# Delta stage of a two-layer bidirectional encoder: the four small-tile phases of the inverse merge grouped into two places of a step

## The chip, the cores and the metric

The kernel runs on one core of a Trainium2 chip. The metric is the device time of one execution in microseconds (us), lower is better; the time given is the median of several executions. Engines are written as in the profile: PE (matrix products), ACT (scalar engine), DVE (vector engine), POOL (GpSimd), SP (the queue that issues most transfers).

## What is computed

Two layers over 2048 tokens of width 1024. Each layer makes one wide input projection, a gated DeltaNet branch that is scanned forward and backward in chunks of 64 tokens, a convolution branch, and a gated merge. The part that the change touches is the chunked delta rule, cut here to what matters:

```python
def gated_delta_chunked(q, k, v, g, beta):
    ...
    lmat = jnp.where(strict, jnp.einsum('bhncd,bhnsd->bhncs', k_beta, k) * decay, 0.0)
    ...
    sol = lax.linalg.triangular_solve(eye + lmat, rhs, left_side=True, lower=True,
                                      unit_diagonal=True)
    ...
    def step(state, inp):
        val_n, kc_n, a_n, qd_n, kd_n, dl_n = inp
        v_new = val_n - jnp.einsum('bhcd,bhde->bhce', kc_n, state)
        o_n = jnp.einsum('bhcd,bhde->bhce', qd_n, state) + jnp.einsum('bhcs,bhse->bhce', a_n, v_new)
        state = state * dl_n[..., None, None] + jnp.einsum('bhcd,bhce->bhde', kd_n, v_new)
        return state, o_n
    ...
o = o_fwd + o_bwd
```

The kernel works on chunks of 128 tokens and needs, for each chunk, head and direction, the inverse of a unit triangular 128x128 matrix. Its 32x32 diagonal blocks have been inverted earlier; the delta stage merges them, first to 64x64 and then to 128x128 blocks.

## The kernel before, in words

**The stage.** `delta` runs 16 steps per layer. Step s treats chunk s forward (direction 0) and chunk 15-s backward (direction 1). It lies once in each of the two layers; in the first layer the steps 1 to 15 begin (first instruction of L967) between 934.8 and 1257.8 us.

**One step.** Two generators `lane`, one for each direction, have four phases: products of the old state with keys and queries (`pk` L967, `pq` L970, 128x128 in float32, four heads each, both directions; DVE takes `pk` at L972, ACT takes `pq` at L976); from step 8 on POOL adds the output of the other direction (L979); the product with the inverse (`pw` L983, copied by ACT at L985); the state update and output (`pn` L992, `po` L1001, taken by DVE at L995 and at L1003 or L1008). From step 9 on `finish` normalizes the two chunks that the step before completed: squares on ACT (L1022), a chain of 14 operations of 128x8 elements on DVE (L1032, L1033, the lines 190 to 196 of `rsqrt`, L1036), a scaling on ACT (L1040), transposes on PE (L1045) and a product on DVE (L1046).

**The preparation of a step's inverse.** The generator `prep(i)` prepares step i in phases, each called with `go(i)`: 0 loads; 1 POOL adds a mask (L885); 2 ACT takes the exponential (L891); 3 DVE transposes, copies and multiplies (L895, L901, L905, L907; ACT copies at L903); 4 `z1`, 16 products of 32x32 (L914) and an ACT copy (L917); 5 `do` and `po`, 24 products of 32x32 (L924, L927) and six DVE copies (L929 to L933); 6 `z2`, 8 products of 64x64 (L938, L939) and an ACT copy (L941); 7 `d2`, 8 products of 64x64 (L947, L948) and two DVE copies (L949, L950). The phases of PE, 4 to 7, each stood alone at one of four places of a step: `z1` behind `pk`/`pq`, `do` behind `pw`, `z2` behind `pn`/`po`, and `d2` before the last stretch of filling.

**The filling.** Between these pieces `pull(n)` runs n units of dense work of the next stage (`gates`, and from step 13 on `early_merge`): a unit is three products of 128x128 by 128x512 (L174, L175, L176, weights split into `whi` on ACT, L157, and `wlo` on DVE, L158). ACT takes a finished tile `pd` at L808. A step pulls 16 units, 4 behind each place. `early_merge` takes its tiles on DVE with a sigmoid of ACT (L1167, L1173).

**What sets the order.** Each engine runs its instructions in the order in which the program issues them; there is no planner here. So a phase that waits on an engine holds up everything issued later on that engine. Five PSUM tiles `pz` are shared by all small products of the stage; a new tile waits until the last reader of the tile before in its slot is done.

```python
STEP = (4, 4, 4, 4)
...
    def pz(self):
        return self.ppz.tile([P, NB], F32, tag="pz", name="pz")
```

Of the kernel before, what the change touches and what calls it, by code (L numbers as in the profile page):

```python
# [27 lines left out]
GAP = 0  # L28
SPLIT = 247
LEAD = (8, 10, 6, 6, 6, 4)  # L30
STEP = (4, 4, 4, 4)
TAIL = (3, 3, 2)
Z = '121'
LATE = 4
# [42 lines left out]
class Trunk:  # L77
# [734 lines left out]
    def delta(self):  # L812
        nc = self.nc
# [6 lines left out]
        def ring(cols, n):  # L820
            out = []
            for _ in range(n):
                slot = next(x for x in left if x[2] - x[1] >= cols)
                out.append(slot[0][:, slot[1]:slot[1] + cols])
                slot[1] += cols
            return Ring(out)

        rkq, rkv = ring(1024, 4), ring(1024, 4)
        rgq, rgk = ring(NB, 6), ring(NB, 4)
        rwt = ring(1024, 3)  # L830
        rgb, ro1, rvn, ro, rza, rst, dp = (ring(NB, n) for n in (4, 2, 2, 5, 2, 2, 2))
# [5 lines left out]
        hv = lambda t: t.rearrange("p (h c) -> p h c", h=4)  # L837

        def fetch(step):
            out = []  # L840
            for d in range(2):
                c = step if d == 0 else NCH - 1 - step
                kq = rkq().rearrange("p (h a c) -> p h a c", h=4, a=2)
                kv = rkv().rearrange("p (a h c) -> p a h c", h=4, a=2)
                self.load(kq, self.kq_d[c])
                self.load(kv, self.kv_d[c])
                out.append((c, kq, kv))
            return out

        def decay_keys(ins, d):  # L850
            c, _, kv = ins
            k2 = col(self.kf, d, c)
            nc.gpsimd.tensor_tensor(out=kv[:, 0], in0=kv[:, 0], in1=k2[:, :, None].to_broadcast([P, 4, P]),
                                    op=ALU.mult)
# [7 lines left out]
        def prep(step):  # L862
            ins, ks, gbs = [], [], []
# [2 lines left out]
            pt = dpt[:, 256:512].rearrange("p (d h c) -> p d h c", d=2, h=4)  # L866
            chunk = (step, NCH - 1 - step)
            for d, c in enumerate(chunk):
                g, k, gb = hv(rgq()), hv(rgk()), hv(rgb())
                with nc.allow_non_contiguous_dma(reason="rows to all partitions and inverse blocks"):  # L870
                    r0 = d * 64 + c * 4
                    self.load(gb, self.gc_d[r0:r0 + 4][None].to_broadcast([P, 4, P]))
                    self.load(k, self.g_d[c][:, :, 0, :])
                    self.load(g, self.g_d[c][:, :, 1, :])
                    r4 = 64 * d + 4 * c
                    self.load((dt if d == 0 else pt)[:, d],
                              self.inv_d[:, r4:r4 + 4, :].rearrange("h b (i j) -> (b i) h j", j=32))
                ins.append(g)
                ks.append(k)
                gbs.append(gb)  # L880
            yield
            for d, c in enumerate(chunk):
                gb = gbs[d]
# [3 lines left out]
            for d, c in enumerate(chunk):  # L887
                gb = gbs[d]
# [10 lines left out]
            for b in range(4):  # L899
                r = blk(b)  # L900
                v_.tensor_copy(wt[r, :, 32 * b:32 * b + 32], dtm[r])  # L901
                d, q = (0, 32 * b) if b < 2 else (1, 32 * (b - 2))
# [150 lines left out]
        def pull(n):  # L1053
            for _ in range(n):
                if next(fill, GAP) == GAP:
                    return

        start = self.mark()
        nil = iter(())
        preps = [prep(i) for i in range(NCH)] + [nil, nil, nil]  # L1060
        go = lambda i: next(preps[i], None)
        go(0)
        ins = fetch(0)
        pull(LEAD[0])
        go(0)
        go(0)
        go(0)
        go(1)
        pull(LEAD[1])
        go(0)  # L1070
# [2 lines left out]
            decay_keys(ins[d], d)  # L1073
        pull(LEAD[2])
        go(1)
        go(0)
        pull(LEAD[3])
        go(1)
        go(0)
        go(2)  # L1080
        pull(LEAD[4])
        ready = go(0)
        pull(LEAD[5])
        last = finish([])
        for step in range(NCH):
            nxt = fetch(step + 1) if step + 1 < NCH else None
            gs, wt = ready
            lanes = [lane(step, d, gs[d], wt, *ins[d]) for d in range(2)]
            for x in lanes:
                next(x)  # L1090
            go(step + 1)
            go(step + 2)
            for x in lanes:
                next(x)
            if nxt:
                for d in range(2):
                    decay_keys(nxt[d], d)
            next(last)
            pull(STEP[0])
            for x in lanes:  # L1100
                next(x)
            go(step + 2)
            next(last)
            go(step + 1)
            pull(STEP[1])
            for x in lanes:
                next(x, None)
            go(step + 1)
            go(step + 2)
            go(step + 3)  # L1110
            new = finish(list(done))
            done.clear()
            next(new)
            pull(STEP[2])
            next(last)
            ready = go(step + 1)
            last = new
            pull(STEP[3])
            ins = nxt
        for n in TAIL:  # L1120
            pull(n)
# [251 lines left out]
```

## Time and profile before

| | |
|---|---|
| median of 3 runs | 3189.29 us (3188.14 to 3192.9) |
| the profiled execution | 3187.47 us, its span 3185.7 us |
| mean granted clock of PE | 0.993 of full speed |
| busy share of the span | PE 97%, DVE 75%, ACT 43%, POOL 9% |

The span is the time from the first to the last instruction that the profiler saw; the 1.8 us between it and the execution's own time lie around it. PE is busy nearly all the time, so the time of the kernel is nearly the time of PE's instructions, plus PE's idle stretches, plus what PE loses when its granted clock falls.

### The profile page before, as it was taken

The page shows a single profiled execution, that of the slowest core. Times are in us where ns is not written, and L with a number is a line of the kernel's source. Part 1 is how long each engine was busy: PE and PEld are TensorE (multiplying, and loading weights), DVE is VectorE, ACT ScalarE, POOL GpSimd, SP SyncE. Part 2 cuts the span into 40 slices and gives each one's busy share as a digit, 9 for nine tenths or more (in the row PEclk, how much of TensorE's full clock was granted, in tenths as well). Part 3 has the DMA queues.
Part 4 walks back from the last instruction along what each step waited for, and adds up shares of the span by engine and source line. Part 5 has one row for each costly group of instructions (what it writes and reads, how often), then busy time and mean ns, then how long its engine had stood idle before and what let it go on. Part 6 is the DMA issues. An engine that isn't in the chain of part 4 may idle for free. (4 is left out here: it accounts for less than half of the span.)

```text
span 3185.7 us, 51259 instructions
## 1 busy us (share of the span) xinstructions
PE 3090.6 (97%) x19110; PEld 2705.8 (85%) x19110; DVE 2398.4 (75%) x4409; ACT 1385.3 (43%) x3104; POOL 302.3 (9%) x297
## 2 busy tenths in 40 slices
PE   6999999999999999999999999999999999999997
PEld 5788888888889998787888888888888999878786
DVE  7789898987646697745676989898955567867655
ACT  5625151522444466533345242425234445655332
POOL 3000000000122231000000000000002222200000
PEclk9999999999999999999999999999999999999999
DMA  4323222334687886654413131414357777855634
GB/s 141 90 96 93 87 93 87 93 112 133 206 288 247 258 267 208 198 185 133 135 53 101 66 120 60 120 60 123 117 186 261 243 252 255 283 182 192 204 126 146
DMA packets 427545, 501.70 MB, mean 157 GB/s; under 512 B 96224, under 2 KB 260704, under 8 KB 427296
## 3 DMA queue, kind: packets, MB, share of 16 engines
q1 hardware_dynamic: 354544, 388.58, 39.2%
q10 hardware_dynamic: 64688, 80.09, 7.3%
q0 software_dynamic: 8064, 29.76, 2.5%
q8 instruction: 150, 2.46, 0.3%
q14 instruction: 99, 0.81, 0.1%
HBM read 342.74 MB, written 155.58 MB: 156 GB/s over the span
## 5 line engine op out<-in xcount | busy, mean ns | idle before, releaser
L174 PE MATMUL pd<-h,whi 128*128 128x512 f32 x2816 | 1092.1, 388 | 0.0
L176 PE MATMUL pd<-h,wlo 128*128 128x512 f32 x2816 | 1070.4, 380 | 1.9 <-DVE wlo L158 1.9
L175 PE MATMUL pd<-h,whi 128*128 128x512 f32 x2816 | 1070.9, 380 | 0.0
L728 DVE SCALAR_TENSOR_TENSOR cacc<-gp,vec,cacc 128x1009 f32<-128x1009 f32 (+1 forms) x480 | 614.3, 1280 | 37.5 <-ACT cacc L726 34.3
L176 PEld LDWEIGHTS pd<-h,wlo 128*128 128x128 f32 x2816 | 533.8, 190 | 79.3 <-DVE wlo L158 3.5
L174 PEld LDWEIGHTS pd<-h,whi 128*128 128x128 f32 x2816 | 534.0, 190 | 79.0 <-issue 1.4
L175 PEld LDWEIGHTS pd<-h,whi 128*128 128x128 f32 x2816 | 534.5, 190 | 72.4 <-issue 1.9
L157 ACT ACTIVATE whi<-wraw 128x512 fp32r<-128x512 f32 x400 | 242.7, 623 | 473.2 <-PE pd L175 335.9
L158 DVE TENSOR_TENSOR wlo<-wraw,whi 128x512 fp32r<-128x512 f32 x400 | 275.0, 701 | 142.1 <-ACT whi L157 141.8
L553 DVE SCALAR_TENSOR_TENSOR acc<-cin,vec,acc 128x1022 f32<-128x1022 f32 (+1 forms) x192 | 246.5, 1299 | 14.4 <-ACT acc L551 13.2
L176 PE MATMUL pd<-yhi,wlo 128*128 128x512 f32 x512 | 194.9, 381 | 3.8 <-DVE wlo L158 3.7
L174 PE MATMUL pd<-yhi,whi 128*128 128x512 f32 x512 | 194.6, 380 | 0.9 <-ACT whi L157 0.9
L175 PE MATMUL pd<-ylo,whi 128*128 128x512 f32 x512 | 194.0, 379 | 0.0
L808 ACT ACTIVATE go<-pd,vec 128x512 f32<-128x512 f32 x128 | 87.1, 680 | 147.9 <-PE pd L176 138.2
L529 ACT ACTIVATE cin<-pd 128x512 f32<-128x512 f32 x96 | 57.0, 594 | 154.7 <-PE pd L176 154.6
L176 PEld LDWEIGHTS pd<-yhi,wlo 128*128 128x128 f32 x512 | 96.8, 189 | 19.9 <-DVE wlo L158 6.4
L740 ACT ACTIVATE ao<-pd 128x512 f32<-128x512 f32 x64 | 38.3, 598 | 170.0 <-PE pd L176 169.9
L174 PEld LDWEIGHTS pd<-yhi,whi 128*128 128x128 f32 x512 | 96.8, 189 | 15.4 <-ACT whi L157 2.0
L175 PEld LDWEIGHTS pd<-ylo,whi 128*128 128x128 f32 x512 | 96.8, 189 | 13.6
L174 PE MATMUL pd<-uop,whi 128*128 128x512 f32 x256 | 101.0, 395 | 6.6 <-ACT whi L157 6.5
L176 PE MATMUL pd<-uop,wlo 128*128 128x512 f32 x256 | 99.1, 387 | 2.3 <-DVE wlo L158 1.4
L175 PE MATMUL pd<-gop,whi 128*128 128x512 f32 x256 | 97.7, 381 | 3.0 <-DVE gop L158 3.0
(297 smaller groups left out, 4754.9 us busy)
## 6 DMA issues: line engine op xcount, KB each, us to landing
wraw<-w_in SPq DMA_DIRECT2D x240, 256.0 KB, 3.3
gt<-go ACTq DMA_DIRECT2D x128, 256.0 KB, 3.6
dl<-gr SPq DMA_DIRECT2D x128, 256.0 KB, 5.2
dl<-kq SPq DMA_DIRECT2D x64, 512.0 KB, 6.1
dl<-kv SPq DMA_DIRECT2D x64, 512.0 KB, 5.8
wraw<-w_out SPq DMA_DIRECT2D x96, 256.0 KB, 3.0
kq<-acc SPq DMA_DIRECT2D x16, 1024.0 KB, 5.5
gr<-go ACTq DMA_DIRECT2D x64, 256.0 KB, 2.2
```

The lines of the kernel that those rows point to most:

```text
L157: self.nc.scalar.activation(hi, src, AF.Copy)
L158: self.nc.vector.tensor_tensor(out=lo, in0=src, in1=hi.bitcast(F32), op=ALU.subtract)
L174: mm(ps, whi[:, k, :], xhi, start=k == 0, stop=False)
L175: mm(ps, whi[:, k, :], xlo, start=False, stop=False)
L176: mm(ps, wlo[:, k, :], xhi, start=False, stop=k == kk - 1)
L529: nc.scalar.activation(cut(t[:, o + b * NB:o + (b + 1) * NB]), sort(ps), AF.Copy)
L553: self.nc.vector.scalar_tensor_tensor(out=out, in0=t[:, k:k + n], scalar=wc(k), in1=out, op0=ALU.mult, op1=ALU.add)
L728: self.nc.vector.scalar_tensor_tensor(out=acc, in0=t[:, k:k + n], scalar=wc(k), in1=acc, op0=ALU.mult, op1=ALU.add)
L740: nc.scalar.activation(cut(o), sort(ps), func)
L808: nc.scalar.activation(cut(o), sort(ps), AF.Identity, bias=self.vec[:, V_GB + j:V_GB + j + 1])
```

## The change

The loads of a preparation are split in two phases (the broadcast row `gb` first, the keys, gates and inverse blocks later), and the phases of preparations are called at other places. With the new numbers of lines (four more than before from L885 on) a step s now holds: behind `pk`/`pq` the exponential of preparation s+2 and 6 units; behind `pw` the DVE phase of s+2, the load of `gb` of s+3 and 5 units; behind `pn`/`po` first `z2` of s+1, then `z1` of s+2, the other loads of s+3 and 5 units; then, before the next step, `do` of s+2, `d2` of s+1 and the mask of s+3, with no filling behind them. The units of a step are 16 as before, and no instruction of PE is added or left out. Before the first step `z2` of 0 stands with `z1` of 1, and `d2` of 0 with `do` of 1.

```diff
-STEP = (4, 4, 4, 4)
+STEP = (6, 5, 5)
...
-                g, k, gb = hv(rgq()), hv(rgk()), hv(rgb())
-                with nc.allow_non_contiguous_dma(reason="rows to all partitions and inverse blocks"):
+                gb = hv(rgb())
+                with nc.allow_non_contiguous_dma(reason="rows to all partitions"):
                     r0 = d * 64 + c * 4
                     self.load(gb, self.gc_d[r0:r0 + 4][None].to_broadcast([P, 4, P]))
+                gbs.append(gb)
+            yield
+            for d, c in enumerate(chunk):
+                g, k = hv(rgq()), hv(rgk())
...
         pull(LEAD[4])
         ready = go(0)
+        go(1)
+        go(2)
         pull(LEAD[5])
...
             for x in lanes:
                 next(x)
-            go(step + 1)
             go(step + 2)
             for x in lanes:
                 next(x)
...
             for x in lanes:
                 next(x)
             go(step + 2)
+            go(step + 3)
             next(last)
-            go(step + 1)
             pull(STEP[1])
...
             pull(STEP[2])
             next(last)
+            go(step + 2)
             ready = go(step + 1)
+            go(step + 3)
             last = new
-            pull(STEP[3])
             ins = nxt
```

PE, the end of an early step, before: `z2` (L938, L939) stands alone, filling follows, then `d2` (L947, L948), filling, and the `pk` of the next step (L967). The first and the last products of each kind are shown.

```order
L1001 MATMUL pz<-dm_6983,dl_6981 128x128 x4
L938 MATMUL pz<-dh_6988,dl_6981 64x64
L939 MATMUL pz<-dh_6988,dl_6981 64x64
L174 MATMUL pd<-h_395,whi 128x512
...
L176 MATMUL pd<-h_395,wlo 128x512
L947 MATMUL pz<-dl_6981,dh_6989 64x64
L948 MATMUL pz<-dl_6981,dh_6989 64x64
L174 MATMUL pd<-h_395,whi 128x512
...
L967 MATMUL pz<-dh_6986,dl_6980 128x128 x4
```

The same place in the changed kernel: `z1` (L918) follows `z2` (L942, L943) at once; after the filling `do`/`po` (L928, L931) and `d2` (L951, L952) stand together, and the next step's `pk` (L971) follows them.

```order
L943 MATMUL pz<-dh_6988,dl_6981 64x64
L918 MATMUL pz<-dh_6988,dl_6981 32x32 x16
L174 MATMUL pd<-h_395,whi 128x512
...
L176 MATMUL pd<-h_395,wlo 128x512
L928 MATMUL pz<-dh_6988,dh_6989 32x32 x4
L931 MATMUL pz<-dh_6989,dh_6988 32x32 x2
L951 MATMUL pz<-dl_6981,dh_6989 64x64
L952 MATMUL pz<-dl_6981,dh_6989 64x64
L971 MATMUL pz<-dh_6986,dl_6980 128x128 x4
```

Four kinds of small place per step have become two, and the copies of ACT and DVE that belong to the second phase of a place come behind those of the first.

DVE, a step from 10 on, before: the chain ends with L1036; then come the copies of `do`, the state update, and only then the DVE phase of the preparation (L895 to L907) and the split of weights.

```order
L1036 TENSOR_TENSOR orr<-orr,cq 128x8
L929 COPY dh_6988<-pz 32x4x32
...
L995 SCALAR_TENSOR_TENSOR dh_6986<-dh_6986,dl,pz 128x128 x4
L1003 TENSOR_TENSOR dm_6984<-pz,dm_6984 128x512
...
L895 STREAM_TRANSPOSE dh_6987<-dh_6987 128x128 x2
L901 COPY dl_6981<-dh_6987 32x8x32 x4
L905 TENSOR_TENSOR dl_6981<-dl_6981,dm_6982 128x512 x2
L907 TENSOR_TENSOR dl_6981<-dl_6981,dm_6982 128x512 x2
L158 TENSOR_TENSOR wlo<-wraw,whi 128x512 x2
L1046 SCALAR_TENSOR_TENSOR dh_6985<-pz,vec,dh_6985 128x512
```

DVE in the changed kernel: the phase of the preparation and the split of weights stand between the chain and the state update, and the copies of `do` and `d2` come last.

```order
L1040 TENSOR_TENSOR orr<-orr,cq 128x8
L899 STREAM_TRANSPOSE dh_6987<-dh_6987 128x128 x2
L905 COPY dl_6981<-dh_6987 32x8x32 x4
L909 TENSOR_TENSOR dl_6981<-dl_6981,dm_6982 128x512 x2
L911 TENSOR_TENSOR dl_6981<-dl_6981,dm_6982 128x512 x2
L158 TENSOR_TENSOR wlo<-wraw,whi 128x512 x2
L999 SCALAR_TENSOR_TENSOR dh_6986<-dh_6986,dl,pz 128x128 x4
L1007 TENSOR_TENSOR dm_6984<-pz,dm_6984 128x512
...
L1050 SCALAR_TENSOR_TENSOR dh_6985<-pz,vec,dh_6985 128x512
...
L933 COPY dh_6988<-pz 32x4x32
```

The state update thus stands behind about 4 us more of DVE's own work than before.

ACT, the same kind of step in the changed kernel: the copy of `z2` (L945) and that of `z1` (L921) are neighbours, behind the copies of the DVE phase (L907), the scaling (L1044), a finished tile (L808) and the split of weights (L157).

```order
L989 ACTIVATE dm_6983<-pz 128x512 x2
L907 ACTIVATE dh_6988<-dh_6988 32x4x32 x4
L1044 ACTIVATE dm_6984<-dm_6984,orr 128x128 x8
L808 ACTIVATE go<-pd,vec 128x512
L151 DMA gt_150<-go 128x512
L157 ACTIVATE whi<-wraw 128x512 x2
L945 ACTIVATE dh_6989<-pz 128x256
L921 ACTIVATE dh_6989<-pz 128x128
L1026 ACTIVATE junk,oss<-dh_6985 128x128 x4
```

Before, the copy of `z1` stood right behind the `pq` copies at the head of the step, two places earlier in the queue.

## Rows read from the trace of the kernel before

**Rows 1.** The page: busy time of each engine; PE's granted clock in 40 slices.

```profile
PE 3090.6 (97%) x19110; PEld 2705.8 (85%) x19110; DVE 2398.4 (75%) x4409; ACT 1385.3 (43%) x3104; POOL 302.3 (9%) x297
...
PEclk9999999999999999999999999999999999999999
```

**Rows 2.** Busy time by stretch, steps 5, 11, 12, 13, 14: bounds, us, PE, PEld, DVE, ACT, POOL, PEclk.

```profile
1023.74:1045.97 22.23, 22.23 (x242) 20.09 (x241) 14.16 (x39) 10.13 (x28) 5.13 (x4) 1.00 0.77 247
...
1158.87:1182.16 23.29, 23.29 (x249) 21.10 (x248) 21.26 (x54) 15.25 (x53) 7.00 (x6) 1.00 0.91 279
1182.16:1205.64 23.48, 23.37 (x249) 21.10 (x248) 22.72 (x57) 14.95 (x52) 7.00 (x6) 1.00 0.92 287
1205.64:1228.75 23.11, 23.11 (x250) 21.03 (x248) 18.85 (x58) 16.97 (x49) 5.05 (x4) 1.00 0.85 285
1228.75:1257.81 29.06, 24.83 (x250) 22.56 (x248) 20.54 (x54) 18.27 (x59) 4.54 (x4) 0.94 0.49 145
```

**Rows 3.** Timeline of PE around one `d2`: start, us, engine, line, tiles, count.

```profile
1042.35 0.38 PE L176 MATMUL pd<-h,wlo 128*128 128x512 f32 x1
1042.66 0.27 PE L947 MATMUL pz<-dl,dh 64*64 64x64 f32 x1
...
1043.12 0.22 PE L947 MATMUL pz<-dl,dh 64*64 64x64 f32 x1
...
1043.27 0.48 PE L174 MATMUL pd<-h,whi 128*128 128x512 f32 x1
1043.59 0.38 PE L175 MATMUL pd<-h,whi 128*128 128x512 f32 x1
1043.81 0.38 PE L176 MATMUL pd<-h,wlo 128*128 128x512 f32 x1
```

**Rows 4.** Timeline of PE: first and last product of the `z2` before.

```profile
1039.26 0.27 PE L938 MATMUL pz<-dh,dl 64*64 64x64 f32 x1
...
1039.72 0.22 PE L938 MATMUL pz<-dh,dl 64*64 64x64 f32 x1
```

**Rows 5.** Timeline of ACT: the copy of that `z2`.

```profile
1040.02 0.39 ACT L941 ACTIVATE dh<-pz 128x256 f32<-128x256 f32 x1 [3.53 <-PE pz L939]
```

**Rows 6.** Timeline of DVE: the state update of direction 0 in that step.

```profile
1036.69 1.12 DVE L995 SCALAR_TENSOR_TENSOR dh<-dh,dl,pz 128x128 f32<-128x128 f32 x4 [1.77 <-PE pz L992]
```

**Rows 7.** Timeline of POOL in step 10 (which begins at 1135.77).

```profile
1142.05 2.04 POOL L853 TENSOR_TENSOR dl<-dl,kf 128x512 f32<-128x512 f32 x2
1144.05 2.50 POOL L885 TENSOR_TENSOR dm<-dm,con 128x512 f32<-128x512 f32 x2
```

**Rows 8.** Timeline of DVE in step 10: three of the 14 operations of the chain.

```profile
1145.37 1.20 DVE L196 SCALAR_TENSOR_TENSOR orr<-rst,orr 128x8 f32<-128x8 f32 x1
1146.61 0.17 DVE L194 TENSOR_TENSOR rst<-orr,rsv 128x8 f32<-128x8 f32 x1
...
1147.82 0.17 DVE L1036 TENSOR_TENSOR orr<-orr,cq 128x8 f32<-128x8 f32 x1
```

**Rows 9.** Timeline of ACT in step 13: scaling, splits, a finished tile.

```profile
1217.20 1.27 ACT L1040 ACTIVATE dm<-dm,orr 128x128 f32<-128x128 f32 x4
...
1219.54 2.18 ACT L157 ACTIVATE uop<-uop 128x512 fp32r<-128x512 f32 x4
1221.62 0.67 ACT L808 ACTIVATE go<-pd,vec 128x512 f32<-128x512 f32 x1
```

**Rows 10.** Timeline of all engines in step 14, around PE's longest wait of the stage.

```profile
1231.56 1.28 ACT L1167 ACT_TABLE_LOAD   x1
...
1233.52 0.69 DVE L1173 TENSOR_TENSOR y<-pd,g 128x512 f32<-128x512 f32 x1 [1.25 <-ACT g L1167]
...
1234.13 1.40 DVE L1046 SCALAR_TENSOR_TENSOR dh<-pz,vec,dh 128x512 f32<-128x512 f32 x2
...
1234.92 0.80 PE L967 MATMUL pz<-dh,dl 128*128 128x128 f32 x2 [4.23 <-DVE dh L1046]
```

**Rows 11.** Busy time by stretch: the 3.5 us behind that wait.

```profile
1234.80:1238.30 3.50, 3.38 (x16) 3.32 (x16) 3.46 (x11) 0.24 (x1) 1.26 (x1) 0.54 0.78 231
```

More of the change, by code (lines that the diff above doesn't have):

```diff
@@ L868, in prep @@
             for d, c in enumerate(chunk):
-                g, k, gb = hv(rgq()), hv(rgk()), hv(rgb())
-                with nc.allow_non_contiguous_dma(reason="rows to all partitions and inverse blocks"):
+                gb = hv(rgb())
+                with nc.allow_non_contiguous_dma(reason="rows to all partitions"):
                     r0 = d * 64 + c * 4
                     self.load(gb, self.gc_d[r0:r0 + 4][None].to_broadcast([P, 4, P]))
+                gbs.append(gb)
+            yield
+            for d, c in enumerate(chunk):
+                g, k = hv(rgq()), hv(rgk())
+                with nc.allow_non_contiguous_dma(reason="inverse blocks"):
                     self.load(k, self.g_d[c][:, :, 0, :])
@@ L879, in prep @@
                 ks.append(k)
-                gbs.append(gb)
             yield
@@ L1062, in delta @@
         go(0)
+        go(0)
         ins = fetch(0)
@@ L1075, in delta @@
         go(1)
+        go(1)
         go(0)
         pull(LEAD[3])
+        go(0)
         go(1)
-        go(0)
+        go(2)
         go(2)
@@ L1082, in delta @@
         ready = go(0)
+        go(1)
+        go(2)
         pull(LEAD[5])
```

## The prediction

> **What bounds the kernel now.** I first read the page's busy times: PE is busy 97% of the span at nearly full clock [rows 1], so time can be won only by making PE's own stream shorter, or lost by making PE wait. Second, the busy times by step [rows 2]: in an early step PE is busy all of 22.23 us, DVE 14.2 and ACT 10.1, so there is slack beside PE. In steps 11 to 13 DVE is busy 18.9 to 22.7 of about 23.3 us; there a delay on DVE or ACT can reach PE. Step 14 is the exception: 29.06 us, of which PE works 24.83. Third, PE's timeline around a small place [rows 3]. The dense products start every 0.22 us. The first `d2` product starts 0.31 us behind the last dense one, 0.09 more than the pitch; the last `d2` product stands 0.15 us before the next dense one, about 0.1 more than the 0.06 or so from one `d2` pair to the next; and that dense product takes 0.32 us until the next starts, 0.1 too much. So each small place pays about 0.3 us for the way in and out, beside its own products.
>
> **Part 1: two places in place of four.** A step loses two ways in and out, 0.6 us, and gets two new changes inside a place, from 64x64 to 32x32 products and back. No row shows such a change. Its bounds are 0 (the small sizes follow each other like products of one size) and 0.3 us (it pays like a whole place). I take 0.15, half of the 0.3 that pays for two changes, one in and one out [rows 3]. So a merged place saves 0.15 us. There are 30 a layer: one of each kind before the first step, 14 of each in steps 0 to 13. 27 of them act freely, by the next part: 27 x 0.15 = 4.05 us a layer.
>
> The Trainium skill, "TensorEngine Tiling (Array Packing)", section Key Properties, says that changing the tiling mode, not just the tile, drains the engine, and 64 by 64 and 32 by 32 are two modes there. By that rule a change inside a place would cost what the rows charge for the whole way, the saving of this part would be nothing, and the sum would be that of the first rival below. The rows agree in that every change of size there costs something.
>
> **Part 2: what `z1` now waits for.** In the merged place `z1` needs a PSUM tile directly behind `z2`. By the instructions' own waits, in steps 1 to 8, 12 and 13 it takes the tile of `pn` of direction 0, which DVE frees with the first state update. In an early step that update starts 1036.69 and lasts 1.12 us, done 1.4 us before `z2` starts at 1039.26 [rows 4, 6]; in the change DVE has the preparation's work ahead of it, but in an early step that fits into the 8 us that DVE has free [rows 2]. So no wait.
>
> In steps 9 to 11 the tile is the one that `z2` itself filled, so `z1` waits for ACT's copy. `z2` takes 0.46 us from its first to its last start, the copy starts 0.76 us after the first start and lasts 0.39 [rows 4, 5]: `z1` starts 1.15 us after `z2` did, 0.69 after its last product. Before, the two phases paid beside their products two ways of 0.3; now one way of 0.3 and this wait of 0.69. That is 0.4 us worse a step, 1.2 a layer, if ACT is free in time. It should be, but barely. In step 10 DVE's chain takes until 1147.99, 12.2 us into the step, since its operations of 0.17 us last up to 1.2 while POOL works [rows 7, 8]; the first short one starts at 1146.61, right behind the end of the masks (1144.05 + 2.50). The change takes the masks, 2.5 us, away from there to the end of the step, so I let the chain end 9.7 us into it. Behind it and two transposes (about 10.5) ACT has four copies (at 0.39 like rows 5: 1.6), eight scalings (four start in 1.17 us: 2.3), a tile of 0.67 and two splits (0.52 each) [rows 5, 9]: done at 16.1. PE reaches `z2` after 11 units of 0.65 us [rows 3] and 8.9 us of float32 products (what 16 units and four places of about 0.75 leave of 22.23 [rows 2]), at 16.0, and ACT's copy is wanted at 16.8. The slack is 0.7 us.
>
> **Part 3: steps 11 and 12.** They last 0.2 and 0.4 us over the 23.1 of step 13 [rows 2], since DVE takes the transposes (L1046) and the splits ahead of the `pk` results. Splits now stand half a step earlier. I count 0.5 us a layer as won.
>
> **Part 4: steps 13 and 14.** Step 14's 29.06 us are 5.9 over the usual 23.1 [rows 2]. PE waited 4.23 us for DVE's L1046, which stood behind a product that waited for a sigmoid, that behind a table load of 1.28 us on ACT, that behind a split and the eight squares; then the clock fell: 0.54 over the next 3.5 us, the lower of the two levels, 1.2 GHz, for nearly all of it [rows 10, 11]. The units moved by the new pulls bring the split (0.5), the table load (1.28) and one sigmoid (0.6 by the 0.69 of L1173's product, which it must follow) to the head of that queue, before the squares. The wait left is about 4.3 - 2.4 = 1.9 us. But the same work now stands ahead of the state update in step 13. After the exponentials, some 7 us into the step, ACT has nine splits (4.7), eight scalings (2.3), six copies (2.3) and a tile (0.67) [rows 5, 9], so the last split ends at 17, its DVE half and the state update (0.6 + 1.1 [rows 6]) at 18.8, and `z1`, which could start at 16.8, starts 2 to 2.5 us late. Together 4.2 of waiting in place of 4.2, and the clock's fall (about 1.6 us) saved if two short waits cost no clock. I count 1.5 us won a layer, with bounds of 5 won and 3 lost.
>
> What has cover: the six copies behind `do` and two behind `d2` on DVE (0.3 to 0.4 each) now run under the next `pk` and delay its results by about 1.2 us; 6 units of 0.65 stand between them and `pw`, which would be the first to wait. The exponential and the masks are half a step early, loads of `gb` likewise. SP's queue keeps its number of transfers; a load of `gb` that waits holds the others behind it, but they are wanted a step later.
>
> **The sum.** Per layer: -4.05 + 1.2 - 0.5 - 1.5 = -4.85 us, two layers -9.7. From the profiled execution's 3187.47 that is 3177.8; the median of the runs lies 1.8 above it, so I say **3180**.
>
> **The rivals.**
> 1. The change of size costs a full way in and out. Part 1 is then 0: +1.2 - 0.5 - 1.5 = -0.8 a layer, about 3188. For it: both changes shown cost something. Against it: the entry and exit of rows 3 are between sizes that differ much, and part of the exit lies in the first dense product.
> 2. The change of size is free and steps 13 and 14 come out at the good end. Part 1 is 8.1 a layer, part 4 about 2: -9.4 a layer, about 3170. For it: within a place the products overlap.
> 3. The other side: ACT is late in steps 9 to 11. It decides when the chain or a split comes more than 0.7 us later than I let it; with the chain at 12.2 us as before, each of these steps waits 1.8 us more, 5.4 a layer. The same lateness costs some 2 more in step 13, and a clock that falls behind each long wait 1.6: -4.85 + 9 = +4.2 a layer, about 3198. For it: DVE has only 2 us free in steps 11 and 12 [rows 2]. Against it: the masks are gone from the chain.
> 4. That the change does not do what it says is excluded for PE by the order of its instructions; what is open is only whether the ways in and out are what it saves.
>
> **How the numbers follow.** About 0.2% (6.4 us) is what a measurement of this kernel can tell from no change; faster means below 3183. My forecast has 0.42, of which a quarter lies above 3183; rival 1 has 0.22, rival 2 0.23, rival 3 0.13. Faster: 0.31 + 0.23 + 0.06 from the better part of rival 1 = 0.60; slower: 0.13; the rest, 0.27, the same. The range goes from rival 2 (3170, less 2 for its bounds) to between rivals 1 and 3, 3194.
>
> **What would show it.** In the changed profile: early steps of about 21.9 us (22.23 - 0.3); 21.6 would be the free change, 22.2 the full one. In steps 9 to 11 an idle PE of about 0.6 us between `z2` and `z1`, waiting for ACT's copy; over 1.5 would be rival 3. In step 13 a wait at `z1` for the state update, and a shorter one at the `pk` of step 14, without a stretch at the lower clock. I am wrong if early steps are not shorter, or if steps 9 to 12 exceed 24 us.

## The result, and the profile after

The changed kernel takes 3203.41 us (median; 3196.58 to 3207.12) against 3192.9 us (3188.14 to 3198.09) for the kernel before, run beside it on the same chip: a ratio of 1.0031, 95% interval 1.0021 to 1.0041. It is slower; 3180 us and a gain had been forecast. The profiled execution took 3196.58 us with a span of 3194.8, 9.1 us more than that of before. It is the fastest of its seven executions: the medians differ by 10.5 us, and the account below is that of the two profiled executions.

The page of the changed kernel, busy times and granted clock (answers to [rows 1]):

```profile
PE 3085.8 (97%) x19110; PEld 2707.5 (85%) x19110; DVE 2436.9 (76%) x4409; ACT 1384.3 (43%) x3104; POOL 318.2 (10%) x297
...
PEclk9999999999999999999999999999999999999999
```

PE was busy for 4.8 us less than before, yet the span is 9.1 longer: PE's idle time grew by 13.9. Busy times by stretch of the changed kernel (bounds, us, then PE, PEld, DVE, ACT, POOL, PEclk, DMA): from the first `z1` before the first step to the `pk` of step 1; a half-clock stretch in it; steps 1, 9, 10, 11, 12, 13, 14; a half-clock stretch in step 13.

```profile
899.60:943.35 43.75, 38.41 (x468) 33.14 (x467) 19.13 (x43) 19.55 (x47) 10.29 (x8) 0.92 0.78 257
...
914.00:918.60 4.60, 4.50 (x54) 3.88 (x55) 1.42 (x5) 0.66 (x2) 3.10 (x3) 0.50 0.76 226
943.35:965.19 21.84, 21.84 (x245) 19.94 (x241) 15.67 (x39) 10.10 (x28) 4.65 (x4) 1.00 0.78 255
...
1118.43:1142.74 24.31, 22.89 (x253) 20.98 (x249) 21.45 (x54) 14.97 (x50) 7.01 (x6) 1.00 0.56 178
1142.74:1166.13 23.39, 22.88 (x252) 20.97 (x249) 22.66 (x55) 14.68 (x49) 8.86 (x6) 1.00 0.89 267
1166.13:1189.52 23.39, 22.88 (x252) 20.98 (x248) 22.66 (x55) 15.30 (x53) 8.84 (x6) 1.00 0.91 281
1189.52:1212.24 22.72, 22.72 (x253) 20.88 (x249) 19.35 (x53) 16.58 (x61) 8.54 (x6) 1.00 0.97 301
1212.24:1242.29 30.05, 25.52 (x253) 22.87 (x249) 24.72 (x64) 21.11 (x62) 4.63 (x4) 0.89 0.82 264
1242.29:1264.30 22.01, 22.01 (x172) 19.94 (x168) 16.40 (x46) 12.69 (x42) 4.56 (x4) 1.00 0.50 152
1233.50:1239.50 6.00, 5.80 (x44) 4.71 (x45) 3.07 (x8) 3.59 (x16) 0.00 (x0) 0.50 0.64 224
```

The stretch ahead of step 1 in the kernel before:

```profile
899.05:934.81 35.76, 35.76 (x388) 30.64 (x387) 21.03 (x43) 18.48 (x45) 10.35 (x8) 1.00 0.92 298
```

That stretch, which the forecast passed over, grew by 8.0 us in the first layer (35.76 to 43.75) and by 8.7 in the second (2454.69 to 2490.45 before, 2457.99 to 2502.42 after). Steps 1 to 14 fell by 2.05 us in the first layer (323.00 to 320.95) and 0.45 in the second. The other 5.1 us of the account came back outside these stretches: 0.6 lost ahead of the first, 3.2 and 2.4 won behind the stage in each layer. In the first layer, 1.2 of what was won is idle time of PE in the first 22.2 us of step 15 that went away; the rest was not followed.

By part, in us per layer. The forecast's 27 places are put where they stand: 4 before step 1, 16 in steps 1 to 8, 3 in steps 9 to 11, 2 each in steps 12 and 13.

| stretch | forecast | layer 1 | layer 2 |
|---|---|---|---|
| to the `pk` of step 1 | 4 x -0.15 = -0.60 | +8.0 | +8.7 |
| steps 1 to 8 | 16 x -0.15 = -2.40 | -2.77 | -3.08 |
| steps 9 to 11 | 3 x -0.15 + 1.2 = +0.75 | +1.58 | +1.60 |
| step 12 and part 3 | 2 x -0.15 - 0.5 = -0.80 | -0.75 | +0.44 |
| steps 13 and 14 | 2 x -0.15 - 1.5 = -1.80 | -0.10 | +0.59 |

**Ahead of step 1.** PE's waits of the changed kernel from 895 to 960 us (engine, line, whom it waited for: us in total, times, longest); the kernel before has none there:

```profile
PE pz L942 <- DVE dh L933: 5.3, 1, 5.3
```

`z2` of the first preparation waits for a copy of its own `do` on DVE. These are the lines of the change that set the order there; the section on the change does not show them:

```diff
         pull(LEAD[2])
         go(1)
+        go(1)
         go(0)
         pull(LEAD[3])
+        go(0)
         go(1)
-        go(0)
+        go(2)
         go(2)
```

The second `go(1)` is the DVE phase of preparation 1, the `go(0)` behind it `do` of 0. DVE in that stretch, changed kernel (start, us, line, tiles, count, in brackets the idle time before and what ended it):

```profile
902.76 0.50 DVE L899 STREAM_TRANSPOSE dh<-dh 128x128 f32<-128x128 f32 x2
903.36 1.18 DVE L905 COPY dl<-dh 32x256 f32<-32x256 f32 x4
909.07 0.85 DVE L909 TENSOR_TENSOR dl<-dl,dm 128x512 f32<-128x512 f32 x1 [4.53 <-ACT dm L895]
...
911.52 2.12 DVE L911 TENSOR_TENSOR dl<-dl,dm 128x512 f32<-128x512 f32 x2
913.67 0.28 DVE L933 COPY dh<-pz 32x128 f32<-32x128 f32 x1
```

The same in the kernel before:

```profile
904.27 0.28 DVE L929 COPY dh<-pz 32x128 f32<-32x128 f32 x1 [1.91 <-PE pz L927]
...
906.13 0.50 DVE L895 STREAM_TRANSPOSE dh<-dh 128x128 f32<-128x128 f32 x2
```

Before, DVE copied `do` of preparation 0 as soon as PE had it (904.27) and then turned to preparation 1. In the changed order the whole DVE phase of preparation 1 stands ahead of that copy. Its product L909 waits 4.53 us for an exponential on ACT, and the copy, whose `do` PE had ended by 904.7, starts at 913.67. Then PE's granted clock is 0.50, the lower level (1.2 GHz), for 4.60 us. The account: 5.3 of waiting, half of 4.6 for the clock, and 0.9 for the `z1` and `do` of one more preparation that now lie ahead of step 1 (468 records of products against 388, two for each small product; 0.38 for a `z1` and 0.55 for a `do` in an early step), less some 0.4 saved: 8.1, against 8.0 measured. The 0.9 comes back in step 14 (172 records against 250).

**Early steps.** PE around the two merged places of step 1:

```profile
960.06 0.22 PE L943 MATMUL pz<-dh,dl 64*64 64x64 f32 x1
960.21 0.45 PE L918 MATMUL pz<-dh,dl 32*32 32x32 f32 x32
...
965.04 0.22 PE L952 MATMUL pz<-dl,dh 64*64 64x64 f32 x1
965.19 1.05 PE L971 MATMUL pz<-dh,dl 128*128 128x128 f32 x7
```

From the last 64x64 product to the first of 32x32 it is 0.15 us, where 64x64 products follow at 0.06: a change inside a place costs about 0.1. The step fell from 22.23 [rows 2] to 21.84, 0.195 per merged place.

**Steps 9 to 13.** PE's waits of the changed kernel from 1090 to 1265 us:

```profile
PE pz L918 <- DVE dh L999: 4.8, 2, 4.5
PE pz L918 <- ACT dh L945: 2.4, 3, 1.4
```

All are waits of `z1` for its PSUM tile: three of 0.5 to 1.4 us in steps 9 to 11 for ACT's copy of `z2`, and 4.5 in step 13 for the state update, followed by 6.0 us at the lower clock. In the second layer those of steps 9 to 11 are the same, and the state update is waited for in step 12 (1.2) and step 13 (5.3). In step 9, POOL and the chain on DVE:

```profile
1124.83 2.03 POOL L853 TENSOR_TENSOR dl<-dl,kf 128x512 f32<-128x512 f32 x2
1126.82 2.50 POOL L889 TENSOR_TENSOR dm<-dm,con 128x512 f32<-128x512 f32 x2
```

```profile
1126.92 1.20 DVE L194 TENSOR_TENSOR rst<-orr,rsv 128x8 f32<-128x8 f32 x1
1128.15 1.21 DVE L195 TENSOR_TENSOR rst<-rst,orr 128x8 f32<-128x8 f32 x1
1129.39 0.17 DVE L196 SCALAR_TENSOR_TENSOR orr<-rst,orr 128x8 f32<-128x8 f32 x1
```

The masks (L889) are issued at the end of the step, but on POOL nothing stands between L853 and them, in the changed kernel as in the one before [rows 7]. So they ran right behind L853, beside the chain, which ended at 1130.36, 11.9 us into the step (11.8 before). In steps 10 and 11 it ended 8.4 to 8.5 us into the step (12.2 and 12.6 before), since there POOL came later: the second L983 waits for a load. Step 10, POOL and the end of the chain:

```profile
1152.61 1.33 POOL L983 TENSOR_TENSOR dm<-dm,dm 128x512 f32<-128x512 f32 x1 [2.86 <-DMA dm<-o]
...
1156.81 3.39 POOL L889 TENSOR_TENSOR dm<-dm,con 128x512 f32<-128x512 f32 x2
```

```profile
1151.02 0.17 DVE L1040 TENSOR_TENSOR orr<-orr,cq 128x8 f32<-128x8 f32 x1
```

And step 13, DVE and one row of ACT:

```profile
1232.53 1.12 DVE L999 SCALAR_TENSOR_TENSOR dh<-dh,dl,pz 128x128 f32<-128x128 f32 x4
...
1240.68 0.69 DVE L1183 TENSOR_TENSOR y<-pd,g 128x512 f32<-128x512 f32 x1 [3.60 <-ACT g L1177]
1241.29 1.40 DVE L1050 SCALAR_TENSOR_TENSOR dh<-pz,vec,dh 128x512 f32<-128x512 f32 x2
```

```profile
1235.72 0.63 ACT L1177 ACTIVATE g<-g 128x512 f32<-128x512 f32 x1 [3.31 <-DMA g<-gt]
```

Two chains set this step. One is `z1`'s wait for the state update (1232.53); from its end, 1233.70, PE reaches the `pk` of step 14 at 1242.29 without a further wait. The other is gate load, sigmoid, eight squares, second sigmoid, second `y` (1240.68) and the products behind the transposes (L1050), the first of which is done by about 1242.0. This trace alone does not tell whether that `pk` would have waited for L1050 without the first wait; e16 below, where the first wait is gone, shows that it does.

### The profile page after: what moved, and what is told of

It reads as the page before. It is cut to its first block, busy times and chain, and to the rows that moved or that the text cites. A ratio compares the mean times of both kernels' runs of the same rounds, so it can differ in the third digit from the quotient of the medians.

```text
span 3194.8 us, 51188 instructions
## 1 busy us (share of the span) xinstructions
PE 3085.8 (97%) x19110; PEld 2707.5 (85%) x19110; DVE 2436.9 (76%) x4409; ACT 1384.3 (43%) x3104; POOL 318.2 (10%) x297
## 5 line engine op out<-in xcount | busy, mean ns | idle before, releaser
L176 PE MATMUL pd<-h,wlo 128*128 128x512 f32 x2816 | 1072.5, 381 | 1.5 <-DVE wlo L158 1.5
L176 PEld LDWEIGHTS pd<-h,wlo 128*128 128x128 f32 x2816 | 534.8, 190 | 78.9 <-DVE wlo L158 3.1
L157 ACT ACTIVATE whi<-wraw 128x512 fp32r<-128x512 f32 x400 | 242.8, 624 | 474.6 <-PE pd L175 332.3
L158 DVE TENSOR_TENSOR wlo<-wraw,whi 128x512 fp32r<-128x512 f32 x400 | 283.8, 723 | 147.9 <-ACT whi L157 147.5
L176 PE MATMUL pd<-yhi,wlo 128*128 128x512 f32 x512 | 194.7, 380 | 3.3 <-DVE wlo L158 3.3
L808 ACT ACTIVATE go<-pd,vec 128x512 f32<-128x512 f32 x128 | 86.9, 679 | 141.4 <-PE pd L176 124.7
L176 PEld LDWEIGHTS pd<-yhi,wlo 128*128 128x128 f32 x512 | 96.8, 189 | 18.9 <-DVE wlo L158 5.3
L853 POOL TENSOR_TENSOR dl<-dl,kf 128x512 f32<-128x512 f32 x64 | 74.7, 1176 | 289.4 <-DMA dl<-kv 245.3
L980 ACT ACTIVATE dm<-pz,eg 128x128 f32<-128x128 f32 x240 | 68.0, 371 | 82.0 <-PE pz L974 74.5
```

Source lines behind the costliest of these rows:

```text
L157: self.nc.scalar.activation(hi, src, AF.Copy)
L158: self.nc.vector.tensor_tensor(out=lo, in0=src, in1=hi.bitcast(F32), op=ALU.subtract)
L176: mm(ps, wlo[:, k, :], xhi, start=False, stop=k == kk - 1)
L808: nc.scalar.activation(cut(o), sort(ps), AF.Identity, bias=self.vec[:, V_GB + j:V_GB + j + 1])
L980: nc.scalar.activation(hv(o1)[:, hd, :], pq[:, hd, :], AF.Copy, scale=eg[:, hd:hd + 1])
```

## The experiments

Three questions were put. Is the loss the DVE order ahead of step 1 (theory lead) or the steps? Are the waits of steps 9 to 12 those for a PSUM tile (theory tile)? Does the tile wait set step 13, or the chain on ACT and DVE (theory chain)? The expectations call theory lead A, with B for a loss in the steps, and theory tile D. Ratios are to the kernel before, run on the same chip, whose medians were 3192.1 to 3194.61 us.

### The stretch ahead of step 1

**e1: the DVE phase of preparation 1 behind `do` of 0.**

```diff
         go(1)
+        go(0)
         go(1)
-        go(0)
```

(Three calls follow `pull(LEAD[2])`: `go(1)`, `go(1)`, `go(0)` in the changed kernel, `go(1)`, `go(0)`, `go(1)` now.)

> The changed kernel with one call moved ahead of the first step: the DVE phase of preparation 1 is issued behind do of preparation 0, not ahead of it. Theory A (the loss lies ahead of step 1: the copies of do of 0 stand on DVE behind products that wait for the exponential of 1, and z2 of 0 waits for them, 5.3 us, with PE at half clock for some 4 us behind it): that wait goes; z1 of 1 may then wait 2 to 3 us for the products of the DVE phase itself. 5 to 14 us faster than the changed kernel over both layers, ratio to before 0.998 to 1.0015. Theory B (the loss is made in steps 9 to 13, the place ahead of step 1 costs little): no faster than the changed kernel, ratio 1.003.

3196.6 us, 1.0015 (1.0007 to 1.0024): half the way. The `z2` wait is gone; PE now waits at `z1` of preparation 1 for its product, and the clock falls behind that too (the profiled execution, 3206.92 us, is the slowest of twelve):

```profile
915.39 0.31 PE L918 MATMUL pz<-dh,dl 32*32 32x32 f32 x2 [2.53 <-DVE dl L909]
```

```profile
915.39:922.00 6.61, 6.31 (x45) 5.06 (x46) 2.47 (x5) 2.11 (x4) 1.67 (x2) 0.52 0.98 300
```

**e2: e1, and four units of the lead's filling moved ahead of that `z1`.**

```diff
-LEAD = (8, 10, 6, 6, 6, 4)
+LEAD = (8, 10, 6, 10, 2, 4)
```

> As the run before, and four units of filling moved from behind z1 of 1 to ahead of z2 of 0 and z1 of 1 (10 and 2 in place of 6 and 6), so that both find their inputs ready. Theory A: no wait of PE over 0.5 us ahead of step 1, step 1 begins about 8 us earlier in each layer than in the changed kernel, 16 us in all: ratio to before 0.997 to 0.999. Theory B: ratio 1.003.

3188.79 us, 0.9987 (0.9979 to 0.9996). The stretch takes 36.65 us at full clock, 0.9 above before, which is the 0.9 of products moved into it:

```profile
902.98:939.63 36.65, 36.27 (x468) 31.42 (x467) 21.28 (x43) 18.45 (x47) 9.21 (x8) 1.00 0.84 281
```

One call moved and one line of numbers give back 14.6 us of the changed kernel's 3203.4, and this version stands below the kernel before.

**e3: the kernel before with only the wrong order.**

```diff
+        go(1)
         go(0)
         pull(LEAD[3])
-        go(1)
```

> The kernel before with one call moved: the DVE phase of preparation 1 is issued ahead of do of preparation 0, as the change does; all places stay apart. Theory A: z2 of 0 waits about 5 us for the first copies of do and PE falls to half clock behind it, 12 to 18 us over both layers: ratio 1.004 to 1.0055. A rival within A (it needs z1 of 1 in the same place too): under 6 us, ratio below 1.002. Theory B: 1.000.

3208.98 us, 1.0051 (1.0038 to 1.0063), with the changed kernel's wait and nothing else of the change:

```profile
PE pz L938 <- DVE dh L929: 5.6, 1, 5.6
```

Theory lead holds from both sides: taking the order away removes the loss, and putting it alone into the kernel before makes one of 16 us.

### Steps 9 to 12

**e4: e2 with less filling ahead of `z1`.**

```diff
-STEP = (6, 5, 5)
+STEP = (4, 4, 8)
```

> The run e2 (mended order ahead of step 1) with the 16 units of a step as 4, 4 and 8 in place of 6, 5 and 5, so that a step's splits of weights (ACT whi, DVE wlo) come behind z1 again as in the kernel before. Theory C (z1's waits in steps 9 to 11 and 13 come from splits that stand ahead of the ACT copy and of the state update): the 2.4 us of waiting in steps 9 to 11 fall below 1.8, the wait of step 13 from 4.7 to about 3.5, but the wait of the pk of step 14 for L1050 comes back with 3 to 4.5 us and half clock behind it: ratio to e2 0.999 to 1.002. A rival (the splits don't matter, only the place does): waits as in e2.

3213.91 us, 1.0068 (1.0054 to 1.0082): steps 9 to 11 of the first layer take 26.6 to 26.9 us. Its waits from 1090 to 1290 us:

```profile
PE pz L918 <- DVE dh L999: 8.4, 4, 2.4
PE pz L918 <- ACT dh L945: 6.1, 1, 6.1
```

The waits were to fall below 1.8 us in steps 9 to 11, with the `pk` of step 14 waiting instead; they rose to 7.0 there, and that `pk` waited 0.75. So splits behind `z1` do not cure the wait when three units (2 us) less stand ahead of it; it fits that the filling ahead of a place is what covers the work of ACT and DVE behind which the tile comes free.

**e7 and e8: six tiles `pz`, two tiles `pd`,** in e2 (e7) and, as a control, in the kernel before (e8).

```diff
-                tc.tile_pool(name="pdn", bufs=3, space=PSUM) as self.ppd, \
-                tc.tile_pool(name="pzz", bufs=5, space=PSUM) as self.ppz:
+                tc.tile_pool(name="pdn", bufs=2, space=PSUM) as self.ppd, \
+                tc.tile_pool(name="pzz", bufs=6, space=PSUM) as self.ppz:
```

> The run e2 with six PSUM tiles for the small products and two for the dense ones, in place of five and three. z1 then takes a tile that pw left, and waits for neither ACT's copy of z2 nor the state update. Theory D (the waits of z1 in steps 9 to 13 are waits for a tile, not for its data): no wait of z1 over 0.3 us in steps 9 to 12; in step 13 z1 starts behind z2 at once or waits for its products (L909) for under 2 us, and the state update is waited for later, by the transposes or do, for less; 2.4 us a layer in steps 9 to 11 and 2 to 5 in step 13 come back: ratio to e2 0.996 to 0.998, less what the dense stages lose with two tiles. Against D: z1 waits as long for its products: ratio 1.000.

> The kernel before with six small and two dense PSUM tiles: the control for e7. If the number of tiles is all that e7 gains by, and in any kernel, this is as much faster than the kernel before as e7 is than e2. By theory D the kernel before has no wait for a tile in steps 1 to 13, so only the dense stages can change: ratio 1.000 to 1.004.

e7: 3220.05 us, 1.0091 (1.0077 to 1.0105); e8: 3227.05, 1.0112 (1.0098 to 1.0126), where 1.004 had been the most expected. The tile taken from the dense work costs far more than the stage has to win, before the stage begins: the `pk` of step 1 comes at 955.61 in e8, 934.81 before. The page of e8 says where; this row stands at 1.9 us in the kernel before:

```profile
L176 PE MATMUL pd<-h,wlo 128*128 128x512 f32 x2816 | 1076.4, 382 | 23.8 <-DVE wlo L158 23.8
```

Inside the stage the reading is clean: steps 9 to 12 of e7 take 22.72, 23.07, 22.88 and 23.07 us without a wait of `z1`. So these waits were for the tile. Step 13 still took 29.74 in the first layer, though its tile wait was gone as well: `do` waited 4.2 us for ACT's copy of `z1`, which stands behind a sigmoid that waits 6.1 us for the gate load: a first sign for theory chain. In the second layer it fell to 24.88 (31.55 in e2), and step 14 rose to 26.24 (21.78), 2.9 of them a wait for L1050. A further run, e4 with six tiles (e10), took 3247.94 us, 1.0175 (1.0161 to 1.0189), far from the expected 0.999 to 1.002 of e7: `z1` waits for no tile there, but up to 1.3 us for its own products (L909), and the next step for L1050, 1.5 us in steps 10 to 12 and 5.8 in step 14.

### Step 13

**e5: e2 with the splits for the next stage four units earlier.**

```diff
-SPLIT = 247
+SPLIT = 243
```

> The run e2 with the eight splits of the next operand begun four units earlier (unit 243 in place of 247), so that fewer of them stand on DVE ahead of the preparation's phase and the state update of step 13. If the 4.5 us wait of z1 in step 13 comes from this queue on DVE, it falls to 2 us or less and the 5.8 us at half clock behind it go: 3 to 5 us a layer faster than e2, ratio to e2 0.997 to 0.998. If it comes from the copies that POOL delays or from the gate load, the wait stays within 1 us of 4.5 us and the ratio to e2 is 1.000.

3194.09 us, 1.0004 (0.9996 to 1.0013). The wait moved: that of `z1` in step 13 fell from 4.7 to 2.7 us, and step 12 grew from 22.7 to 27.9. From 1190 to 1270 us:

```profile
PE pz L918 <- DVE dh L999: 4.3, 2, 2.7
PE pz L971 <- DVE dh L1050: 3.5, 1, 3.5
```

**e12 and e13: e2 with `z1` behind the last filling,** from step 9 on (e12), in step 13 alone (e13).

```diff
+            late = step >= 9
...
-            go(step + 2)
+            if not late:
+                go(step + 2)
...
+            if late:
+                go(step + 2)
+                next(last)
+                ready = go(step + 1)
+                go(step + 2)
...
```

> The run e2 with z1 of the steps from 9 on behind the last filling, ahead of the transposes, d2 and do (z1, transposes, d2, do): 3.2 us later than in e2. By the tile theory the waits of steps 9 to 11 (2.4 us a layer) go; the wait of step 13 falls by 3.2 us, to 1.5 in layer 1 and 3.3 in layer 2, and most of the half clock behind it goes; one more way in and out per step costs 0.2 to 0.3, 1.3 a layer. do now waits for ACT's copy of z1, which must stand ahead of ACT's squares: 0 to 1 us a step. Together 3 to 6 us a layer faster than e2, ratio to e2 0.996 to 0.998.

> As e12, in step 13 of each layer alone. The waits of steps 9 to 11 stay; step 13 gains 3.2 us and part of the half clock behind its wait, 3 to 5 us a layer: ratio to e2 0.997 to 0.998. If only the place of the wait moves (the next to wait is the transposes or the pk of step 14), step 13 stays at 29.5 us and the ratio to e2 is 1.000.

e12: 3241.51 us, 1.0157 (1.0144 to 1.017); e13: 3194.66, 1.0003 (0.9991 to 1.0016); e12 had been expected 6 to 12 us below e2. In e12 ACT's copy of `z1` came to stand behind the eight squares, and `do` waited for it, 23.1 us in five waits of the first layer. In e13 steps 13 and 14 of the first layer took 30.2 and 24.6, 3.5 more than in e2: the wait was moved, not removed.

**e11: e2 with 7 units ahead of `z1`** in place of 5, and two fewer in the lead: `z1` comes behind the same units as in e2, but two units (1.3 us) later in its step.

```diff
-LEAD = (8, 10, 6, 10, 2, 4)
-STEP = (6, 5, 5)
+LEAD = (8, 10, 6, 10, 2, 2)
+STEP = (6, 7, 3)
```

> The run e2 with 6, 7 and 3 units in a step (6, 5, 5 in e2) and two units fewer ahead of the first step: pn/po, z2 and z1 come 1.3 us later in a step, so DVE and ACT have 1.3 us more before z1 asks for a tile. If z1's waits are a lateness of the queues on DVE and ACT against a fixed point of PE, each falls by 1.3 us: those of steps 9 to 11 (0.5, 0.5, 1.4) to 0.1 or less, that of step 13 (4.7 in layer 1, 6.5 in layer 2) to 3.4 and 5.2: 3.5 us a layer, ratio to e2 0.997 to 0.9985. If DVE's state update moves along with pn, the waits stay and the ratio to e2 is 1.000.

3188.56 us, 0.9993 (0.9981 to 1.0005), no different from e2: in the first layer ACT's waits of steps 9 to 11 are gone (steps 10 and 11 take 22.72 and 22.93), the state update's are longer (6.5 in total: 1.7 in step 9, 4.8 in step 13).

**e16: e2 in which `z1` shares the tile of the `z2` ahead of it.** The copy of `z2` (ACT) is issued behind `z1`'s products.

```diff
-            pz = self.pz()
-            z1 = pz[:, 0:128].rearrange("p (h c) -> p h c", c=32)
-            po = pz[:, 128:256].rearrange("p (h c) -> p h c", c=32)
+            pz = shared.pop() if shared else self.pz()
+            z1 = pz[:, 256:384].rearrange("p (h c) -> p h c", c=32)
+            po = pz[:, 384:512].rearrange("p (h c) -> p h c", c=32)
...
+            if step < NCH - 1:
+                shared.append(pz)
...
+            go(step + 1)
```

**e17: the same with the fillings and the lead of e11. e18: e17 with the load of the first gate block issued earlier.**

> The kernel with the mended lead in which z1 and po of a step write the second half of the PSUM tile in which z2 of the next step stands, so that z1 waits for no tile to come free, only for the product of its own preparation. Theory tile (step 13 takes 30 us because z1 waits 4.7 us for a tile that the fork splits hold, and the clock falls behind that wait): the z1 wait goes, step 13 falls to 24 to 26 us, the small waits of steps 9 to 11 go as well, and the time falls by 8 to 12 us against the version with the mended lead (3188.8), to about 3178. Theory chain (step 13 ends when the gate load, the sigmoid, the squares, the second sigmoid, y and the copies behind the transposes have run on ACT and DVE): the z1 wait goes but the first product of step 14 waits as long for the transposes of step 13, step 13 stays above 28 us, and the time stays within 3 us of 3188.8.

> The same shared tile with fillings of 6, 7 and 3 blocks and a shorter last part of the lead; the second y of step 13 no longer stands ahead of the copy behind the transposes on DVE. Theory tile: like the run with the shared tile alone, step 13 at 24 to 26 us and a time within 2 us of that run. Theory chain: 2 to 4 us per layer better than that run, because one product of 0.6 us and what it waits for leave the chain; step 13 at 26 to 28 us.

> The same with the load of the first gate block moved ahead, to the place of the first merge weights. Theory tile: no difference to the run before it, within 1 us. Theory chain: the sigmoid no longer waits 3.3 us for its load, squares and the second sigmoid move up by 2 to 3 us, and so does the first product of step 14: 2 to 3 us per layer, 4 to 6 us in all.

e16: 3184.95 us, 0.998 (0.997 to 0.999). e17: 3171.95, 0.9935 (0.9922 to 0.9947). e18: 3177.43, 0.9952 (0.9939 to 0.9966). Waits of e16 in steps 13 and 14 (L976 is `pk`, L1055 the product behind the transposes, L930 `do`, L923 the copy of `z1`):

```profile
PE pz L976 <- DVE dh L1055: 3.6, 1, 3.6
PE pz L930 <- ACT dh L923: 2.5, 1, 2.5
```

`z1` waits for no tile, and step 13 still takes 31.10 us: as theory chain had it for this run, though the time fell by 3.8 us, not by under 3 (by the ratios 2.2, with intervals that overlap). Steps 9 to 11 are 3.5 and 3.3 us shorter than in e2 in the two layers, about half of it lost clock behind the wait of step 9 in e2; steps 13 and 14 are 4 longer in the first layer and as long in the second. With the fillings of e11 on top, the same two edits that gave 4 and 0 us alone, neither clear of the noise, give 17 together; from e16 to e17 it is 13, where theory chain had 4 to 8. From 1197 to 1226 us, e17:

```profile
PE pz L1054 <- DVE dh L1004: 2.3, 1, 2.3
```

Step 13 takes 27.22 us there (28.39 in the second layer). e18 told nothing about the gate load, since in e17 it had already landed when ACT came to it; it came out 5.5 us above e17, not 4 to 6 below, with intervals that overlap, and why was not followed.

**e19: e16 with only the gate load earlier. e20: e16 with only the fillings 6, 7, 3** (the lead as in e2).

> The version with the shared tile (fillings of 6, 5 and 5 blocks) with the load of the first gate block issued earlier. If the gate load is what holds the chain of step 13 there (its sigmoid stood 4.6 us idle for it, the copy of z1 stood behind that sigmoid, and the squares behind both), do no longer waits for the copy of z1 (2.5 us), the squares, the second y and the copy behind the transposes move up by about 4 us, and the first product of step 14 no longer waits 3.6 us: step 13 falls from 31 to 25 or 26 us, and the time by 8 to 12 us, to about 3175. If the place of the second y and the splits in front of the state update set the chain, step 13 falls by at most 2 us and the time by at most 4.

> The version with the shared tile and fillings of 6, 7 and 3 blocks, the lead as in the version with the mended lead, so that the second y still stands ahead of the copy behind the transposes. If the second y on the chain is what costs, the first product of step 14 waits 2 to 4 us and the time is 4 to 8 us above the version in which it stands behind (3172). If it is the filling of 7 blocks ahead of z1 (which gives DVE and ACT 1.3 us more), the time is within 3 us of 3172.

e19: 3184.35 us, 0.9967 (0.9955 to 0.9979), against 3184.95 of e16. The gate is in time and `do` no longer waits 2.5, but the second `y` still stands behind the second sigmoid, which stands behind the squares, and `pk` waits 4.7 for the product behind it. DVE in e19:

```profile
1230.28 0.69 DVE L1191 TENSOR_TENSOR y<-pd,g 128x512 f32<-128x512 f32 x1 [3.42 <-ACT g L1185]
1230.89 1.40 DVE L1055 SCALAR_TENSOR_TENSOR dh<-pz,vec,dh 128x512 f32<-128x512 f32 x2
```

e20: 3175.1 us, 0.9937 (0.9921 to 0.9954). Here the filling of 7 puts both sigmoids on ACT ahead of the squares, and `pk` does not wait; but the first `y` now stands ahead of the state update on DVE and waits for its sigmoid, that for the gate load, and the transposes wait for the update (the profiled execution, 3179.12 us, is the slowest of four):

```profile
1227.12 0.69 DVE L1190 TENSOR_TENSOR y<-pd,g 128x512 f32<-128x512 f32 x1 [3.45 <-ACT g L1184]
1227.72 1.11 DVE L1004 SCALAR_TENSOR_TENSOR dh<-dh,dl,pz 128x128 f32<-128x128 f32 x4
```

So the load is not what ends the chain in e16; the second sigmoid's place behind the squares is. e17 puts the first `y` behind the state update as well (its transposes wait 2.3 us, not 4.8), and has the lowest median: 20.4 us below the kernel before run beside it. The fillings alone account for most of the step from e16 to e17; the ratios of e20 and e17 do not differ by more than their intervals.

## Why the prediction was wrong

**The step that failed** is in part 1: "There are 30 a layer: one of each kind before the first step", of which 27 "act freely, by the next part". The next part examines the waits of steps only; the queues ahead of the first step were never read, nor does "What has cover" name the DVE phase of preparation 1, which the change puts in front of the copies of `do` of 0. That stretch was booked as a gain of 0.6 us with step 0 and lost 8.0 and 8.7. None of the three rivals had it. With it mended (e2) the time is 3188.8, still above 3180, so a second term was wrong too. By the table, steps 9 to 14 missed their forecast by 7.1 us over both layers: 4.1 in steps 13 and 14 (part 4), 1.7 in steps 9 to 11 (part 2), 1.3 in step 12 (part 3).

**Part 1, the way in and out: right, a little small.** 0.15 us per merged place was forecast, 0.195 measured; early steps take 21.84 where "about 21.9" was to be seen. Rivals 1 (22.2) and 2 (21.6) fall. The rule weighed there, from the Trainium skill, "TensorEngine Tiling (Array Packing)", section Key Properties, that a change of mode drains the engine, agrees in that the change shows (0.15 against 0.06); read as costing a whole way it would have left the step at 22.23, and the measurement decides against that.

**Part 2: right in steps 10 and 11, too cheap in step 9.** The forecast let the chain end 9.7 us into the step, since the masks go "away from there to the end of the step". They went there in the program, not on POOL, where they follow L853 as before, and the chain ended at 11.9 in step 9: `z1` waited 1.4 us, not 0.6. In steps 10 and 11 the chain ended at 8.4 to 8.5 and the wait was the 0.5 of the copy alone, but by luck: not the move of the masks but a load that held POOL kept it off the chain. Step 9 met rival 3's condition; its price was too high (5.4 us a layer, where the three waits came to 2.4 and no clock fell behind them in this trace). The limit I had set, "if steps 9 to 12 exceed 24 us", was passed by step 9 alone.

**Part 3: right in the first layer** (step 12 at 22.72), not in the second (23.93), where `z1` waited 1.2 us for the state update.

**Part 4, steps 13 and 14: mechanism right, price wrong.** The forecast had `z1` "2 to 2.5 us late"; it waited 4.5, and the clock fell, which the forecast allowed to be saved. Between the chain and the update the DVE queue held ten splits, eight of them of the next stage's operand, and four copies slowed beside POOL (3.34 us, 1.18 in the kernel before). And the chain of sigmoids did not shorten: the second sigmoid stayed behind the squares. The pair of steps came out 0.1 us shorter in the first layer and 0.6 longer in the second, with 0.9 us less to do. The experiments on step 13 show why each cure alone gave little: two chains end there close together, and removing either leaves the other.

## What to carry to other kernels

When a change reorders phases in a loop, read the queue of every engine in the prologue as well: there a phase that has cover in the loop stands bare, and one operation that waits for another engine holds up a short copy that PE needs. Where two chains end at the same place, edits that give 0 and 4 us apart (within the noise) can give 17 together, so a small result of one does not close the case. Ask of each moved instruction not where it is issued but what stands ahead of it on its engine.

## What the runs showed of the hardware

- PE's granted clock fell to 0.50 behind waits of 5.3 and 4.5 us (for 4.6 and 6.0 us) and, in e1, to 0.52 on the mean of 6.6 us behind one of 2.5; wait and lost clock together cost 1.4 to 2.3 times the wait. The length of a wait alone does not decide it: behind the 1.4 us of step 9 the clock stayed at 1.00 in the changed kernel (24.31 us for the step), and behind the same 1.4 us it fell in e2, whose step 9 reads:

```profile
1114.73:1140.71 25.98, 24.57 (x252) 22.17 (x249) 21.43 (x54) 16.59 (x57) 7.01 (x6) 0.93 0.59 184
```

- Operations of DVE on 128x8 elements in the chain last 0.17 us alone and 0.96 to 1.27 beside POOL (L983, L853, L889 in step 9), and the first one behind POOL's last end (1129.32) starts at 1129.39 and takes 0.17 again. The Trainium skill, "SBUF — State Buffer", section SBUF: two separate sides, says that the two engines share a pair of ports under an exclusive lock: of a GpSimd operation and a DVE operation that has two inputs in SBUF or runs in a two-port mode, whichever starts first holds it for its whole instruction, and the other blocks. The rows agree: in step 9 a slowed operation lasts about as long as one of POOL's, 1.0 us in L853 and 1.25 in L889.
- One PSUM tile fewer for the dense products costs 20.8 us in the 955 us ahead of the stage (e8). Waits for split weights (L176 for DVE's `wlo`) grew by 21.9 us in the whole span, 10.6 of them ahead of 900 us (0.7 to 11.3); the rest of the loss was not followed.
